# A low-rank update on one core: nine and sixteen tiles in one load each, and the first group's work dealt anew

## The chip, the cores and the metric

The kernel runs on one core of one Trainium2 chip. Its time is the device time of one execution in microseconds (us). "Before" is the median of three runs. The profile shows one further execution; its span goes from the first to the last instruction, and its device time is a little longer than the span.

## The reference

x has 16 x 512 = 8192 rows (tokens) of 768 float32 values. A is 768 x 16, B is 16 x 768, and scale is 0.5.

```python
def reference(x, A, B, scale):
    lora = np.matmul(np.matmul(x, A), B)
    return (x + scale * lora).astype(np.float32)
```

Each row of x is projected to 16 numbers by A, these are raised to 768 numbers again by B, and half of that is added to the row. x is read once and the result written once, 25.2 MB each way.

## The kernel before

**Tiles, parts, groups.** A tile is 128 rows of x. The 64 tiles are cut into five parts of 9, 7, 16, 16 and 16 tiles (`PARTS`); in a part each of the 128 partitions holds consecutive rows, so a load of a whole part takes one contiguous piece of memory per partition. x stays in `x_all` (48 tiles of room, named x_sb in the profile); the fifth part goes where the first two were, once they have been stored. The compute goes by groups of eight tiles, numbered 0 to 7, and a group is summed in four pairs of tiles.

**One group's way.** ACT and POOL each narrow four tiles of x to float16 (`narrowed`, L186 to L196, into `xn`). DVE transposes the group in blocks of 32 x 32 (`turned`, L248, into `xt`). PE projects it with 24 matmuls (`projected`, L278, into y_ps, shown as ps_yt), in two halves of 12. ACT scales and spreads the result into block-diagonal `y_bd` with four instructions (L238). PE raises each pair with four matmuls (`raised`, L293, into one of two `lora` buffers), and DVE adds the pair to x in place (`summed`, L252). In the loop on PE (L324 to L331) the order is: raise pairs 0 and 1 of a group, the first half of the next group's projection, raise pairs 2 and 3, the second half.

**Order.** Each engine's work is written out by hand in a function of its own, and semaphores join them. `s_load` counts landed loads, `s_narrow` narrowed halves, `s_turned` transposed groups, `s_taken` that PE has read weights and data of a projection's second matmul (then `xn` and `xt` may be written again), `s_y` finished projections, `s_spread` finished spreads, `s_lora` raised pairs, `s_free` pairs whose lora buffer has been read, `s_sum` the last sum of groups 1, 3, 5 and 7 (`STORED`). Since an instruction of DVE raises one semaphore, the pair behind `s_sum` gets its `s_free` from SP, in SP's `summed` (L141).

**SP issues every transfer**, in this order: load 0 (2 tiles), load 1 (7 tiles), three small loads for A, one for B, load 2 (7), loads 3 and 4 (8 each, the third part), load 5 (16). Then it waits for `s_sum` of group 1 and for ten raised pairs, that is two pairs of group 2 (L169), and issues store 0 (9 tiles) and store 1 (7). As these two land, the loads of the fifth part follow, 8 tiles each. Then come stores 2, 3 and 4 (16 tiles each), each when its groups are summed; store 2 waits besides until PE has begun to raise group 5 (`s_raise`, L181).

**The first group** is dealt by hand. POOL narrows tiles 0 and 1 as load 0 lands, ACT tiles 2 and 3 and then 4 to 7 as load 1 lands. POOL narrows B (`b_half`, L212), and PE spreads it over the partitions (L315), from which ACT makes `b_mm` (L231). DVE transposes A (L243), and POOL makes the projection's weights of it (`w_one` L214, `w_bd` L220). DVE transposes the first group in two halves (L261 to L264).

Of the kernel before, what the change touches and what calls it, by code (L numbers as in the profile page):

```python
# [13 lines left out]
PARTS = [9, 7, 16, 16, 16]  # L14


GROUP = 8

SUB = 4
# [5 lines left out]
SETS, SET = 3, 4  # L25
# [3 lines left out]
def kernel(  # L29
# [19 lines left out]
    NG = sum(PARTS) // GROUP  # L49
    PAIRS = GROUP // 2  # L50
# [4 lines left out]
    def sb(name, shape, dtype):  # L55
        return nc.alloc_sbuf_tensor(name, shape, dtype).ap()
# [13 lines left out]
    b_rows = sb("b_rows", [P, D], fp32)  # L70
    b_half = sb("b_half", [P, D], MM_DT)
# [11 lines left out]
    def sem(name):  # L83
        sems.append(nc.alloc_semaphore(name))
        return sems[-1]
# [10 lines left out]
    def memory(t2, i, s, n):  # L96
        S = PARTS[i]
        return t2[ds(parts[i], S * P), :].rearrange("(p s) d -> p s d", s=S)[:, ds(s, n), :]

    def held(i, s, n):  # L100
        return tiles(where.index((i, s)), n)

    def tiles(t, n):
        return x_all[:, ds(t % ROOM, n), :]

    LOADS = [
        (0, 0, 2), (0, 2, 7), (1, 0, 7), (2, 0, 8), (2, 8, 8), (3, 0, 16), (4, 0, 8), (4, 8, 8)
    ]
    s_load = [sem(f"s_load{k}") for k in range(len(LOADS))]

    def load_of(t):
        i, s = where[t]
        return next(k for k, ld in enumerate(LOADS) if ld[0] == i and ld[1] <= s < ld[1] + ld[2])

    assert SETS * SET == NC
    s_a, s_b = sem("s_a"), sem("s_b")
    s_ready, s_brows, s_pick = sem("s_ready"), sem("s_brows"), sem("s_pick")
    s_w, s_bh, s_bp, s_bm = sem("s_w"), sem("s_bh"), sem("s_bp"), sem("s_bm")
    s_first, s_narrow, s_turned, s_taken = sem("s_first"), sem("s_narrow"), sem("s_turned"), sem("s_taken")
    s_y, s_spread, s_lora = sem("s_y"), sem("s_spread"), sem("s_lora")  # L120

    s_free = [sem(f"s_free{p}") for p in range(PAIRS)]
    s_out0, s_out1, s_raise = sem("s_out0"), sem("s_out1"), sem("s_raise")

    s_sum, s_out = sem("s_sum"), sem("s_out")

# [1 line left out]
    STORES = [(0, 0, 9), (1, 0, 7), (2, 0, 16), (3, 0, 16), (4, 0, 16)]  # L128

    STORED = [where.index((i, s + n - 1)) // GROUP for i, s, n in STORES]  # L130
    assert STORED[0] == STORED[1]

    section = ExitStack()
    section.enter_context(tc.tile_critical(no_gpsimd_drain=True))  # L134
# [1 line left out]
    def on_sync(e):  # L136
        def load(k):
            ld = LOADS[k]
            e.dma_start(out=held(*ld), in_=memory(x2, *ld)).then_inc(s_load[k], 16)  # L139

        def summed(k):  # L141
            e.wait_ge(s_sum, sorted(set(STORED)).index(STORED[k]) + 1)
            if STORED[k] + 1 < NG:

                e.sem_inc(s_free[PAIRS - 1], 1)

        def store(k, done):
            st = STORES[k]
            e.dma_start(out=memory(out2, *st), in_=held(*st)).then_inc(done, 16)

        load(0)
        load(1)
        e.wait_ge(s_ready, 1)
        blocks = A.rearrange("(c e) r -> c (e r)", e=64)
        for c in range(SETS):
            e.dma_start(
                out=a_rows[c : SET * SET : SET, :], in_=blocks[ds(c * SET, SET), :]
            ).then_inc(s_a, 16)
        e.wait_ge(s_brows, 1)
        e.dma_start(out=b_rows[0 : R * APART : APART, :], in_=B).then_inc(s_b, 16)  # L160
        for k in range(2, len(LOADS) - 2):
            load(k)

        for p in range(2, PAIRS):
            e.sem_inc(s_free[p], 1)
        summed(0)


        e.wait_ge(s_lora, 2 * PAIRS + 2)  # L169
        store(0, s_out0)  # L170
        store(1, s_out1)
        e.wait_ge(s_out0, 16)
        load(len(LOADS) - 2)
        e.wait_ge(s_out1, 16)
        load(len(LOADS) - 1)
        for k in range(2, len(STORES)):
            summed(k)
            if k == 2:


                e.wait_ge(s_raise, 6)  # L181
            store(k, s_out)

    here = set()
# [1 line left out]
    def narrowed(e, copy, g, first, n=SUB):  # L186
        t = g * GROUP + first
        for k in dict.fromkeys(load_of(t + k) for k in range(n)):
            if (e, k) not in here:
                here.add((e, k))  # L190
                e.wait_ge(s_load[k], 16)
        if g:
            e.wait_ge(s_taken, g)
        ins = copy(out=xn[:, ds(first, n), :], in_=tiles(t, n))  # L194

        ins.then_inc(s_narrow if g else s_first if first else s_a, 1)  # L196

    def on_gpsimd(e):
        e.memset(a_rows[0:Q], 0.0).then_inc(s_ready, 1)  # L199
        e.memset(b_rows, 0.0).then_inc(s_brows, 1)  # L200
        e.memset(pick, 0.0).then_inc(s_pick, 1)
        e.memset(w_bd.rearrange("p c k m -> p (c k m)").bitcast(fp32), 0.0)  # L202
        e.memset(y_bd.rearrange("p s m -> p (s m)").bitcast(fp32), 0.0).then_inc(s_ready, 1)  # L203
        e.wait_ge(s_pick, 1)
        e.affine_select(  # L205
            out=pick, in_=pick, compare_op=mybir.AluOpType.not_equal, fill=1.0, base=0,
            pattern=[[0, NQ], [-APART, Q]], channel_multiplier=1,
        ).then_inc(s_pick, 1)
        narrowed(e, e.tensor_copy, 0, 0, SUB // 2)
        e.wait_ge(s_pick, 2)  # L210
        e.wait_ge(s_b, 16)
        e.tensor_copy(out=b_half, in_=b_rows).then_inc(s_bh, 1)  # L212
        e.wait_ge(s_ready, 3)
        e.tensor_copy(  # L214
            out=w_one.rearrange("i (c e) k r -> i c e (k r)", c=SETS),
            in_=a_t[0:Q].rearrange("i k r (e c) -> i c e (k r)", c=SET)[:, 0:SETS, 0:SET, :],
        ).then_inc(s_w, 1)
        e.wait_ge(s_w, 1)
        for b in range(NQ):
            e.tensor_copy(  # L220
                out=w_bd[ds(b * Q, Q), :, :, ds(b * Q, R)], in_=w_one
            ).then_inc(s_w, 1)
            e.wait_ge(s_w, b + 2)
        for g in range(1, NG):
            narrowed(e, e.tensor_copy, g, SUB)

    def on_scalar(e):
        narrowed(e, e.copy, 0, SUB // 2, SUB // 2)
        narrowed(e, e.copy, 0, SUB)
        e.wait_ge(s_bp, 1)  # L230
        e.copy(out=b_mm, in_=lora[0][:, 0, :]).then_inc(s_bm, 1)  # L231
        for g in range(NG):
            if g + 1 < NG:
                narrowed(e, e.copy, g + 1, 0)
            e.wait_ge(s_y, g + 1)
            for b in range(NQ):
                q = ds(b * Q, Q)
                last = e.mul(out=y_bd[q, :, q], in_=y_ps[q, :, :], mul=sc)  # L238
            last.then_inc(s_spread, 1)

    def on_vector(e):
        e.wait_ge(s_a, SETS * 16 + 1)
        e.transpose(  # L243
            out=a_t[0:Q].rearrange("i k r c -> i (k r) c"),
            in_=a_rows[0:Q].rearrange("c (i k r) -> c (k r) i", k=2, r=R),
        ).then_inc(s_ready, 1)

        def turned(first, n):  # L248
            ts = [v[:, ds(first, n), :].bitcast(fp32) for v in (xt, xn)]
            return e.transpose(out=ts[0], in_=ts[1])  # L250

        def summed(g, p):  # L252
            xs = tiles(g * GROUP + 2 * p, 2)
            e.wait_ge(s_lora, g * PAIRS + p + 1)
            ins = e.tensor_tensor(out=xs, in0=xs, in1=lora[p % 2], op=mybir.AluOpType.add)  # L255
            if p + 1 == PAIRS and g in STORED:
                ins.then_inc(s_sum, 1)
            elif g + 1 < NG or p + 2 < PAIRS:
                ins.then_inc(s_free[p], 1)

        for h in range(2):  # L261
            e.wait_ge(s_first, h + 1)
            ins = turned(h * SUB, SUB)
        ins.then_inc(s_turned, 1)  # L264
        for g in range(NG):
            if g + 1 < NG:
                e.wait_ge(s_y, g + 1)
                e.wait_ge(s_narrow, 2 * (g + 1))  # L268
                turned(0, GROUP).then_inc(s_turned, 1)
            for p in range(PAIRS):  # L270
                summed(g, p)

    def on_tensor(e):
# [19 lines left out]
        def raised(p):  # L293
            if p == 0:
                e.wait_ge(s_spread, 1)
            free = s_free[(p + 2) % PAIRS]
            e.wait_ge(free, 1)
            t = lora[p % 2]
            mms = []
            for k in range(2):  # L300
                for n0, w in ((0, 512), (512, 256)) if k == 0 else ((0, 256), (256, 512)):
                    mms.append(e.matmul(  # L302
                        t[:, k, ds(n0, w)], y_bd[:, 2 * p + k, :], b_mm[:, ds(n0, w)],
                        start=True, stop=True,
                    ))
            if p == 0:
                mms[0].then_inc(s_raise, 1)
                mms[2].then_inc(s_spread, -1)
            mms[1].then_inc(free, -1)
            mms[-1].then_inc(s_lora, 1)  # L310
# [73 lines left out]
```

## Time and profile before

| What | Value |
|---|---|
| time, median of three runs | 123.47 us (123.42 to 123.60) |
| time of the profiled execution | 123.43 us |
| its span | 121.6 us |
| read from and written to memory | 25.26 MB and 25.17 MB, 415 GB/s over the span |
| busy: DVE, PE, ACT, POOL | 67%, 41%, 31%, 23% of the span |
| one pair's sum on DVE (L255) | 1.735 us, 32 times |
| one group's transposition on DVE (L250) | 3.365 us, 7 times, and two halves of 1.75 us |
| narrowing of four tiles | 2.75 us on ACT and on POOL |
| spread of y on ACT (L238) | four instructions of 0.37 us |

Transfers by time of issue and of landing, in us of the span:

| Transfer | Tiles | Issued | Landed |
|---|---|---|---|
| load 0 | 2 | 0.97 | 5.5 |
| load 1 | 7 | 1.42 | 12.1 |
| load 2 | 7 | 4.57 | 18.6 |
| load 3 | 8 | 5.18 | 25.9 |
| load 4 | 8 | 5.66 | 33.2 |
| load 5 | 16 | 6.15 | 47.8 |
| store 0 | 9 | 44.45 | 55.9 |
| store 1 | 7 | 44.85 | 62.5 |
| load 6 | 8 | 55.95 | 69.7 |
| load 7 | 8 | 62.52 | 77.0 |
| store 2 | 16 | 74.47 | 91.5 |
| store 3 | 16 | 82.67 | 106.2 |
| store 4 | 16 | 100.64 | 120.7 |

How to read it: the busy shares are averages over the span. A transfer's issue is an instruction on SP; its bytes then go through 16 transfer engines, each with its own queue, and a transfer has landed when all 16 have reported. Where the landing of one follows the one before by the time that its bytes take, the engines had no pause between them. The clock that PE was granted stands in the profile as PEclk, in tenths of full speed or as a share; a matmul takes twice as long at half the clock.

### The profile page before, as it was taken

How to read it: one execution, taken by the hardware profiler on the slowest of the kernel's cores; microseconds unless marked ns; L12 is line 12 of the kernel's file. 1: busy time of each engine (PE TensorE's matmuls, PEld its weight loads, DVE VectorE, ACT ScalarE, POOL GpSimd, SP SyncE). 2: the span in 40 equal slices, each digit the busy share in tenths (PEclk: the TensorE clock that was granted, in tenths of full speed). 3: DMA queues.
4: the chain of work that ended last, by engine and by line, in shares of the span. 5: the costliest groups of instructions: out<-in, count | busy, mean ns of one | idle time of the engine just before them, and what ended most of it. 6: DMA issues, size and time to landing. Idle time of an engine off the chain costs nothing.

```text
span 121.6 us, 884 instructions
## 1 busy us (share of the span) xinstructions
PE 49.8 (41%) x322; PEld 29.2 (24%) x322; DVE 81.7 (67%) x42; ACT 37.4 (31%) x43; POOL 28.4 (23%) x24
## 2 busy tenths in 40 slices
PE   0000209487457547746745734774674320000000
PEld 0000006253223424424423322442442110000000
DVE  0000970599999999999999989999995990000000
ACT  4000967626408312735340093643004000000000
POOL 7730567126009002605300080620000000000000
PEclk9999999999999999999999999999999995555555
DMA  3999999999999897999999999998999899899890
GB/s 63 437 431 457 446 398 469 404 420 469 437 517 420 356 517 336 427 421 410 446 416 436 428 428 485 420 517 372 404 517 404 372 517 404 372 517 404 372 517 0
DMA packets 1928, 50.43 MB, mean 415 GB/s; under 512 B 236, under 2 KB 236, under 8 KB 392
## 3 DMA queue, kind: packets, MB, share of 16 engines
q1 hardware_dynamic: 1928, 50.43, 97.0%
HBM read 25.26 MB, written 25.17 MB: 415 GB/s over the span
## 4 chain that ended last, share of the span: by engine, by line
DVE 33%; DMA 29%; PE 9%; ACT 6%; POOL 2%; issue 2%; SPq 0%; DVEq 0%
DVE x_sb L255 21%; DMA x_sb<-in_x_dram 20%; DVE xt L250 12%; DMA out_dram<-x_sb 9%; PE ps_yt L281 6%; ACT xn L194 3%; PE lora_ps L302 3%; ACT y_bd L238 2%; POOL xn L194 2%; SPq L139 0%; SPq L379 0%; DVEq L268 0%; SPq L134 0%
## 5 line engine op out<-in xcount | busy, mean ns | idle before, releaser
L255 DVE TENSOR_TENSOR x_sb<-x_sb,lora_ps 128x1536 f32<-128x1536 f32 x32 | 53.7, 1735 | 1.4 <-PE lora_ps L302 1.4
L194 ACT CAST xn<-x_sb 128x3072 f16<-128x3072 f32 (+1 forms) x9 | 23.4, 2609 | 35.9 <-DMA x_sb<-in_x_dram 24.8
L302 PE MATMUL lora_ps<-b_mm,y_bd 128*128 128x512 f16 (+1 forms) x128 | 25.0, 328 | 22.6 <-ACT y_bd L238 14.3
L194 POOL CAST xn<-x_sb 128x3072 f16<-128x3072 f32 (+1 forms) x8 | 20.7, 2586 | 43.9 <-DMA x_sb<-in_x_dram 24.6
L250 DVE STREAM_TRANSPOSE xt<-xn 128x3072 f32<-128x3072 f32 (+1 forms) x9 | 27.1, 3006 | 5.3 <-PE ps_yt L281 4.4
L281 PE MATMUL ps_yt<-xt,w_bd 128*128 128x256 f16 x192 | 25.2, 282 | 12.2 <-DVE xt L250 12.2
L281 PEld LDWEIGHTS ps_yt<-xt,w_bd 128*128 128x128 f16 x192 | 18.5, 99 | 19.7 <-issue 15.4
L302 PEld LDWEIGHTS lora_ps<-b_mm,y_bd 128*128 128x128 f16 x128 | 10.6, 97 | 35.5 <-ACT y_bd L238 16.6
L238 ACT ACTIVATE y_bd<-ps_yt 32x256 f16<-32x256 f32 x32 | 12.0, 374 | 18.7 <-PE ps_yt L281 18.4
L243 DVE STREAM_TRANSPOSE a_t<-a_rows 32x1024 f32<-32x1024 f32 x1 | 2.0, 1955 | 12.2 <-DMA a_rows<-in_A_dram 12.2
L315 PE MATMUL lora_ps<-b_half,pick 128*128 128x512 f16 (+1 forms) x2 | 0.8, 500 | 13.5 <-POOL b_half L212 13.5
L315 PEld LDWEIGHTS lora_ps<-b_half,pick 128*128 128x128 f16 x2 | 0.1, 105 | 13.5 <-issue 13.5
L212 POOL CAST b_half<-b_rows 128x768 f16<-128x768 f32 x1 | 0.8, 827 | 5.5 <-DMA b_rows<-in_B_dram 5.5
L220 POOL COPY w_bd<-w_one 32x384 f16<-32x384 f16 x4 | 2.0, 500 | 0.2
L194 ACT ACT_TABLE_LOAD x1 | 1.3, 1283 | 0.9 <-SPq L134 0.9
L202 POOL MEMSET w_bd<- 128x1536 f32 x1 | 1.4, 1372 | 0.0
L214 POOL CAST w_one<-a_t 32x384 f16<-32x384 f32 x1 | 0.9, 857 | 0.9 <-DVE a_t L243 0.9
L199 POOL MEMSET a_rows<- 32x1024 f32 x1 | 0.9, 941 | 0.5 <-SPq L134 0.5
L231 ACT CAST b_mm<-lora_ps 128x768 f16<-128x768 f32 x1 | 0.8, 798 | 0.0
L200 POOL MEMSET b_rows<- 128x768 f32 x1 | 0.7, 728 | 0.0
L203 POOL MEMSET y_bd<- 128x512 f32 x1 | 0.5, 514 | 0.0
L205 POOL TENSOR_SCALAR_AFFINE_SELECT pick<-pick 128x128 f16<-128x128 f16 x1 | 0.3, 298 | 0.0
(5 smaller groups left out, 0.6 us busy)
## 6 DMA issues: line engine op xcount, KB each, us to landing
out_dram<-x_sb SPq DMA_DIRECT2D x3, 6144.0 KB, 20.1
x_sb<-in_x_dram SPq DMA_DIRECT2D x4, 3072.0 KB, 17.6
x_sb<-in_x_dram SPq DMA_DIRECT2D x1, 6144.0 KB, 41.6
x_sb<-in_x_dram SPq DMA_DIRECT2D x2, 2688.0 KB, 12.4
out_dram<-x_sb SPq DMA_DIRECT2D x1, 3456.0 KB, 11.5
out_dram<-x_sb SPq DMA_DIRECT2D x1, 2688.0 KB, 17.7
x_sb<-in_x_dram SPq DMA_DIRECT2D x1, 768.0 KB, 4.5
a_rows<-in_A_dram SPq DMA_DIRECT2D x3, 16.0 KB
```

The lines of the kernel that those rows point to most:

```text
L194: ins = copy(out=xn[:, ds(first, n), :], in_=tiles(t, n))
L199: e.memset(a_rows[0:Q], 0.0).then_inc(s_ready, 1)
L202: e.memset(w_bd.rearrange("p c k m -> p (c k m)").bitcast(fp32), 0.0)
L214: e.tensor_copy(out=w_one.rearrange("i (c e) k r -> i c e (k r)", c=SETS), in_=a_t[0:Q].rearrange("i k r (e c) -> i c e (k r)", c=SET)[:, ...
L220: e.tensor_copy(out=w_bd[ds(b * Q, Q), :, :, ds(b * Q, R)], in_=w_one).then_inc(s_w, 1)
L238: last = e.mul(out=y_bd[q, :, q], in_=y_ps[q, :, :], mul=sc)
L243: e.transpose(out=a_t[0:Q].rearrange("i k r c -> i (k r) c"), in_=a_rows[0:Q].rearrange("c (i k r) -> c (k r) i", k=2, r=R),).then_inc(s_r ...
L250: return e.transpose(out=ts[0], in_=ts[1])
L255: ins = e.tensor_tensor(out=xs, in0=xs, in1=lora[p % 2], op=mybir.AluOpType.add)
L281: mm = e.matmul(y_ps, w_bd[:, c, k, :], xv[:, :, c, :, k], start=(m == 0), stop=(m == MMS - 1),)
L302: mms.append(e.matmul(t[:, k, ds(n0, w)], y_bd[:, 2 * p + k, :], b_mm[:, ds(n0, w)], start=True, stop=True,))
L315: last = e.matmul(lora[0][:, 0, ds(n0, w)], pick.rearrange("p b r -> p (b r)"), b_half[:, ds(n0, w)], start=True, stop=True,)
```

## The change

- The first part's nine tiles come as one load in place of two and seven, and the third part's 16 tiles as one in place of eight and eight. There are six loads of x and not eight.
- In the first group ACT narrows tiles 0 to 3 and POOL tiles 4 to 7, one instruction each. ACT, not POOL, narrows B. DVE waits for ACT's half and then for POOL's, which now counts in `s_narrow`; so each later wait on `s_narrow` is for one more.
- On ACT, the narrowing of group 2 comes behind the spread of group 1, and not ahead of it.
- On DVE, the first pair of group 1 is summed ahead of the transposition of group 2.
- On SP, store 0 waits for the third projection (`s_y` at 3) and neither for group 1's last sum nor for raised pairs; that sum is waited for behind it, ahead of store 1. Store 2 waits for the sixth projection (`s_y` at 6), and `s_raise` is gone.

```diff
     LOADS = [
-        (0, 0, 2), (0, 2, 7), (1, 0, 7), (2, 0, 8), (2, 8, 8), (3, 0, 16), (4, 0, 8), (4, 8, 8)
+        (0, 0, 9), (1, 0, 7), (2, 0, 16), (3, 0, 16), (4, 0, 8), (4, 8, 8)
     ]
...
-    assert STORED[0] == STORED[1]
+    assert STORED[0] == STORED[1] == 1 and PARTS[0] <= GROUP + 2
...
         load(0)
-        load(1)
         e.wait_ge(s_ready, 1)
...
-        for k in range(2, len(LOADS) - 2):
+        for k in range(1, len(LOADS) - 2):
             load(k)
...
-        summed(0)
-        e.wait_ge(s_lora, 2 * PAIRS + 2)
+        e.wait_ge(s_y, 3)
         store(0, s_out0)
+        summed(1)
         store(1, s_out1)
...
-                e.wait_ge(s_raise, 6)
+                e.wait_ge(s_y, 6)
...
-        ins.then_inc(s_narrow if g else s_first if first else s_a, 1)
+        ins.then_inc(s_narrow if g or first else s_first, 1)
...
     def on_gpsimd(e):
...
-        narrowed(e, e.tensor_copy, 0, 0, SUB // 2)
-        e.wait_ge(s_pick, 2)
-        e.wait_ge(s_b, 16)
-        e.tensor_copy(out=b_half, in_=b_rows).then_inc(s_bh, 1)
+        narrowed(e, e.tensor_copy, 0, SUB)
...
     def on_scalar(e):
-        narrowed(e, e.copy, 0, SUB // 2, SUB // 2)
-        narrowed(e, e.copy, 0, SUB)
+        narrowed(e, e.copy, 0, 0)
+        e.wait_ge(s_b, 16)
+        e.copy(out=b_half, in_=b_rows).then_inc(s_bh, 1)
...
         for g in range(NG):
-            if g + 1 < NG:
+            if g + 1 < NG and g != 1:
                 narrowed(e, e.copy, g + 1, 0)
...
             last.then_inc(s_spread, 1)
+            if g == 1:
+                narrowed(e, e.copy, g + 1, 0)
...
     def on_vector(e):
-        e.wait_ge(s_a, SETS * 16 + 1)
+        e.wait_ge(s_a, SETS * 16)
...
         for h in range(2):
-            e.wait_ge(s_first, h + 1)
+            e.wait_ge(s_narrow if h else s_first, 1)
             ins = turned(h * SUB, SUB)
         ins.then_inc(s_turned, 1)
         for g in range(NG):
+            ahead = 1 if g == 1 else 0
+            for p in range(ahead):
+                summed(g, p)
             if g + 1 < NG:
                 e.wait_ge(s_y, g + 1)
-                e.wait_ge(s_narrow, 2 * (g + 1))
+                e.wait_ge(s_narrow, 2 * (g + 1) + 1)
                 turned(0, GROUP).then_inc(s_turned, 1)
-            for p in range(PAIRS):
+            for p in range(ahead, PAIRS):
                 summed(g, p)
...
             if p == 0:
-                mms[0].then_inc(s_raise, 1)
                 mms[2].then_inc(s_spread, -1)
```

More of the change, by code (lines that the diff above doesn't have):

```diff
@@ L122 @@
     s_free = [sem(f"s_free{p}") for p in range(PAIRS)]
-    s_out0, s_out1, s_raise = sem("s_out0"), sem("s_out1"), sem("s_raise")
+    s_out0, s_out1 = sem("s_out0"), sem("s_out1")
     s_sum, s_out = sem("s_sum"), sem("s_out")
```

## The prediction, made before the changed kernel was run

> **What bounds the kernel now.** I first looked at section 2 and 3 of the page, since 50 MB move through one core.
>
> ```profile
> PEclk9999999999999999999999999999999995555555
> DMA  3999999999999897999999999998999899899890
> ...
> q1 hardware_dynamic: 1928, 50.43, 97.0%
> ```
>
> The transfer engines are busy from the first slice to the last but one, while the busiest compute engine, DVE, is busy for 67%. The packet records say the same: from the first packet at 1.98 us to the first engine's end at 119.2 no engine is without one. So the span is 1.98 us of start, 118.7 us of gapless transfers (the last store lands at 120.70) and 0.9 us of tail. Whatever leaves this queue full leaves the time as it is; a hole in it is added. So I next asked how late each issue may come. All five stores and the last two loads are issued from SP while an earlier transfer still runs. The chain of waits shows which work sets them:
>
> ```profile
> 42.95 1.49 PE lora_ps L302 x8
> 44.44 0.02 issue
> 44.45 11.48 DMA out_dram<-x_sb
> 55.93 0.02 issue
> 55.95 13.71 DMA x_sb<-in_x_dram
> ...
> 93.86 6.75 DVE x_sb L255 x4
> ```
>
> Store 0 goes out at 44.45, when PE has raised two pairs of group 2; the engines run out of loads between 46.5 and 47.3 (packet records). From an issue to its packets I have one row with an empty queue: the first load, issued at 0.97, whose packets begin on the 16 engines at 1.98 to 2.4, one at 2.7. So an issue is needed 1.0 to 1.7 us ahead: store 0 by about 45.4. Store 2 goes at 74.47 (engines free from 75.7), the last at 100.64 (free from 104.7).
>
> Third, the timeline around group 1 and 2, where the change works:
>
> ```profile
> 31.44 1.53 ACT L238 ACTIVATE y_bd<-ps_yt 32x256 f16<-32x256 f32 x4 [2.18 <-PE ps_yt L281]
> ...
> 33.03 1.47 PE L302 MATMUL lora_ps<-b_mm,y_bd 128*128 128x512 f16 x8 [1.62 <-ACT y_bd L238]
> 35.73 6.71 DVE L255 TENSOR_TENSOR x_sb<-x_sb,lora_ps 128x1536 f32<-128x1536 f32 x4
> ...
> 35.95 1.50 PE L281 MATMUL ps_yt<-xt,w_bd 128*128 128x256 f16 x12 [1.45 <-DVE xt L250]
> ```
>
> DVE is the pace of the compute: a transposition (3.29 from start to start) and four sums (1.66 each) make 9.92 us a group, and PE waits for it 1.45 us. Last, PE's clock, by stretches of 3.41 us (why this width, below; the columns after the stretch are its length, the busy time and count of PE, PEld, DVE, ACT, POOL, then the granted clock):
>
> ```profile
> 72.44:75.86 3.42, 1.47 (x8) 0.70 (x8) 3.29 (x1) 1.50 (x4) 0.02 (x1) 1.00 0.95 410
> ...
> 96.34:99.75 3.41, 0.98 (x5) 0.31 (x4) 3.41 (x3) 0.00 (x0) 0.00 (x0) 1.00 0.97 418
> 99.75:103.16 3.41, 0.00 (x0) 0.00 (x0) 0.86 (x1) 0.00 (x0) 0.00 (x0) 0.50 0.97 418
> ```
>
> The clock is halved at 99.75, only 1.6 us after the last matmul ended (98.16), behind a stretch with 0.98 us of matmuls. Stretches with 1.47 us kept it. The full clock came at 21.24 (the distance between two L281 matmuls falls there from 213 to 112 ns), and from there to 99.75 are 78.51 us, 23 times 3.413: that is where my width comes from.
>
> **Part 1: fewer, larger loads.** Per engine, eight packets of 6 KB and eight of 21.5 KB (0.231 and 0.796 us each from start to start) become eight of 27.6 KB (1.022): 8.21 - 8.17 = 0.04 us. Sixteen of 24.6 KB (0.910) become eight of 49 KB (1.812): 0.06. Two completion records fewer: 0.03. Sum -0.13 us, all on the path. The first packets also cost 0.67 us per engine over their later price, the latency of an empty queue; a larger first packet may hide from none to all of it. I take none: the first packet of each engine was the slow one in nearly all cases.
>
> **Part 2: the first group dealt anew.** ACT narrows four tiles in one go (2.75) from 12.1, and POOL the other four, instead of 4.13 on ACT beside 1.46 early on POOL. ACT then makes b_half (0.80 to 0.83) and b_mm (0.80) until 17.4, before its next tile's input at 18.5. POOL ends its four at 14.9, then w_one (0.86) and w_bd (2.18): 18.0 instead of 17.35. DVE's second half-transposition can begin at 16.6 and ends at 18.4, not 18.06. So the first projection starts 0.2 us later. That delay alone costs nothing: store 0 had 0.9 us to spare.
>
> **Part 3: the third part as one load.** Its first half landed at 25.9 (issued 5.18, 20.7 to landing); now all of it lands where the second half did, 33.2 (5.66 + 27.6), less 0.1. ACT and POOL cannot narrow group 2 before (26.5 until now): 33.2 + 2.75 = 35.95. Behind ACT's narrowing stands nothing of group 1, since its spread of y is moved ahead of it (33.2). DVE sums the pair moved ahead, when raised, at 34.1 to 35.8, then transposes group 2 from 36.0 to 39.4, instead of to 35.8. Now DVE is about 3 us behind, and with the full clock everything follows: projections done at 43.6 to 43.9 (first half from 39.5, 1.5; raises 2 and 3, 0.65 each; second half 1.5), group 1 summed at 45.2, the last sum near 103.0 instead of 100.6 (0.4 us of old idle time at 72.2 taken up). The moved waits fit that: store 0 on the third projection at 43.7, store 1 at 45.2, store 2 on the sixth projection at 73.8, the last store at 103.0, all earlier than the engines run out. Behind SP's new wait stands its credit for the last pair, wanted by PE at 46. With this the sum would be 123.43 - 0.13 = 123.3.
>
> **But PE stands idle.** Its last matmul before the wait ends at 34.7 (raises 0 and 1 of group 1 from 33.25, 1.47), its next starts at 39.5: 4.8 us, with 1.6 us of idle time ahead of those raises too. The longest gap in the trace of before is 2.98 us (71.07 to 74.05). However the 3.41 us stretches fall, one of them holds under 1.0 us of matmuls here: a stretch starting between 33.7 and 37.1 does, and that is nearly a full stretch of starting points. So I expect the half clock at 39.5. At it an L281 matmul takes 213 ns for 112, so the 24 projections and 8 raises behind the transposition (4.4 us of warm work) go at half pace until a stretch was busy enough: 0.89 of one was, at 21.24. A stretch that begins in the wait ends too early to be busy enough, so this takes a whole stretch and up to part of a second from 39.5: 3.4 to 5.4 us, say 4.6, of which half is lost: 2.3 (1.7 to 2.7; 1 if the drop falls behind 39.5 or the return needs little).
>
> [...]
>
> **The sum.** (a) Third projection at 43.7 + 2.3 = 46.0, so store 0's packets at 47.0 to 47.7, the engines free at 46.4 to 47.2: a hole of 0.65 us (0 to 1.2). The first packet behind an empty queue costs more, as at the start, where it was 0.67; a store reads its first bytes from x_sb and not from memory, so between 0 and 0.67, and I take 0.3. (b) Raises 2 and 3 come late for DVE too: raise 2 ends near 43.4 (39.5 + 2.6 + 1.3) instead of 41.8, so the next sum begins 1.6 us later, and its chain is 1.1 to 1.6, say 1.5, further behind. Store 2 at 75.3, packets at 76.3 to 77.0 against engines free at 75.6 to 76.4 and, behind (a), 0.95 later: nothing, up to 0.3. (c) Last sum at 103.0 + 1.5 = 104.5, packets 105.5 to 106.2, against 104.6 to 105.4 and 0.95 later: 0.15 on average (0 to 0.5), since the engine that is served last need not be the one that is free last. Together 0.65 + 0.3 + 0.15 = 1.1, less 0.13: +1.0 us. The profiled execution took 123.43 (span 121.6 and 1.83 around it), 0.04 under the median of 123.47. **Forecast: 124.4 us**, own range 123.75 to 125.6 (from no hole but the late last store, to 5.4 us of half clock, the slow end of 1.0 to 1.7 us and 0.67 for the first packets).
>
> **Rivals.** Measurements of this kernel tell 0.2%, 0.25 us, from no change.
> 1. The clock stays full, or is back within 2 us, so that store 0 is in time. It stays full if only a stretch without any matmul halves it: 4.8 us hold a whole one of 3.41 for (4.8 - 3.41) / 3.41 = 41% of the places where it can begin, so most executions would miss it. For it: the bound between 0.98 and 1.47 us rests on one drop. Against it: that drop came behind a stretch with matmuls. Then 123.3, within 0.2%; 15%.
> 2. The other side: the same, and the larger first packets hide the start. Per engine 0.67 us is at stake; 0.13 + 0.2 to 0.67 gives 122.6 to 123.1, faster. It decides once over 0.12 us of the start is saved. For it: second packets were also slow on four engines (609 to 993 ns for 234), as if small packets outran their descriptors. Against: first packets alone hold most of it; 15%.
> 3. The clock stays low through the whole of the 4.4 us of work: third projection at 43.7 + 4.4 = 48.1, the hole at store 0 is 2.8 us, with the first packet 3.1, less 0.13: 126.4. It decides if the return needs a busier stretch than the 0.89 at 21.24, and PE's half-speed work for a group (10.2 us against DVE's 9.92) would supply that; 8%, counted with slower.
>
> **How the numbers follow.** Forecast 62%, rival 3 8%: slower 70%; same 15%, faster 15%. The range 123.1 to 125.6 leaves out most of rival 2 and of 3.
>
> **What would show it.** L281 matmuls near 213 ns apart around 40 us and two more clock changes; L250's transposition of group 2 at 36.0 to 39.4; store 0's issue near 46.0; a slice around 47 us with a low DMA share; the last sum near 104.5. I am wrong if the clock stays full through 40 us, if a store issued that late still finds its engines busy, or if the first load lands well before 11.9.

## The result, and the profile after

| | before | changed |
|---|---|---|
| median of the runs | 123.55 us (123.42 to 123.6, 6 runs) | 125.25 us (124.21 to 126.22, 6 runs) |
| ratio, 95% interval | | 1.0104 [1.0078, 1.013] |
| profiled execution | 123.43 us | 125.27 us |
| last store lands, in the span | 120.70 us | 122.41 us |

The changed kernel is slower by 1.0%, 1.3 us. The comparison leaves disturbed runs out, so its ratio lies below that of the medians. The runs of the changed kernel lie at 124.2 to 124.3 and at 125.2 to 125.3 (one at 126.22); the trace is of 125.27, so what it explains is 1.84 us, of which 1.71 is the later landing of the last store.

First the page of the changed kernel: the granted clock and the busy share of the transfer engines in 40 slices of 3.08 us, and the queue's share.

```profile
PEclk9999999999999689999999999999999999655555
DMA  4998999899799986999989999979997996996990
...
q1 hardware_dynamic: 1640, 50.43, 96.3%
```

The queue carries the same 50.43 MB in 288 packets fewer, and is full for 96.3% of a longer span. Packets are counted where they start, so a low slice is only a hint. The packet records do not name the engine, but each packet can be followed to the next by its end; by them the 6 of the sixteenth slice (46.2 to 49.3 us) is a hole, while in the two 6s near the end (slices 34 and 37) no engine stands empty. Just ahead of the hole the clock falls, in the fourteenth slice. The timeline of the changed kernel (start, busy time, engine, operation, and in brackets the idle time ahead and what ended it) shows what leads there:

```profile
19.16 5.00 PE L285 MATMUL ps_yt<-xt,w_bd 128*128 128x256 f16 x24 [1.94 <-DVE xt L250]
...
33.13 1.53 ACT L235 ACTIVATE y_bd<-ps_yt 32x256 f16<-32x256 f32 x4 [7.40 <-PE ps_yt L285]
33.88 2.75 POOL L193 CAST xn<-x_sb 128x3072 f16<-128x3072 f32 x1 [11.23 <-DMA x_sb<-in_x_dram]
34.68 2.75 ACT L193 CAST xn<-x_sb 128x3072 f16<-128x3072 f32 x1
...
37.54 3.38 DVE L250 STREAM_TRANSPOSE xt<-xn 128x3072 f32<-128x3072 f32 x1 [0.21 <-ACT xn L193]
...
41.06 2.72 PE L285 MATMUL ps_yt<-xt,w_bd 128*128 128x256 f16 x12 [4.88 <-DVE xt L250]
...
44.74 3.42 DVE L255 TENSOR_TENSOR x_sb<-x_sb,lora_ps 128x1536 f32<-128x1536 f32 x2 [2.19 <-PE lora_ps L306]
...
46.72 1.88 SPq L149 DMA_DIRECT2D out_dram<-x_sb  x2
```

PE waits 4.88 us for the transposition of group 2, and the 12 matmuls behind that wait take 2.72 us, for 1.50 with the full clock. DVE then waits another 2.19 us for raised pairs. The third projection ends at 46.69, and SP issues store 0 at 46.72, 2.3 us later than before. Windows of one clock stretch each (length, busy time and count of PE, PEld, DVE, ACT, POOL, granted clock, DMA share, GB/s), and one of the hole:

```profile
37.39:40.80 3.41, 0.00 (x0) 0.00 (x0) 3.26 (x1) 0.04 (x1) 0.00 (x0) 1.00 1.07 461
40.80:44.21 3.41, 3.15 (x14) 2.08 (x15) 1.76 (x2) 2.52 (x1) 2.49 (x1) 0.50 1.03 447
...
46.00:47.00 1.00, 0.69 (x7) 0.36 (x4) 1.00 (x2) 0.27 (x1) 0.00 (x0) 1.00 0.12 49
```

A whole stretch passes without a matmul; the next one is granted half the clock, and the one behind it the full clock again. From 46 to 47 only 49 GB/s move. By the packet records 15 of the transfer engines stand empty there for 0.36 to 1.18 us; the sixteenth, the last to finish its loads (47.92), does not pause. The mean of the 16 is 0.72. A second loss does not show as a hole. At 60.6 to 63 us the engines turn from store 1 to the load behind it, and their packets there take 0.87 us more than usual (mean of the 16 engines; before 0.16):

```profile
61.00:62.00 1.00, 0.49 (x5) 0.46 (x6) 1.00 (x2) 0.07 (x1) 0.04 (x1) 1.00 1.42 344
62.00:63.00 1.00, 1.00 (x10) 0.62 (x7) 1.00 (x2) 1.00 (x1) 1.00 (x1) 1.00 0.65 221
```

Those two rows carry 344 and 221 GB/s; the same two microseconds of before carry 436 and 418. Since packets are counted where they start, a share may pass 1.

The 1.71 us are then: the start 0.15 later, the hole 0.72, the turn 0.72 more than before, a small hole at 77 us 0.07, fewer packets -0.13, and 0.18 that these terms leave over. (It is no wider spread of the engines' ends: they lie 0.58 us apart, for 1.02 before.) The compute side gives the same answer. The last sum ends at 105.87, 5.26 us later than before: 1.68 from the start (the first projection is that much later at its end), and 3.77 from DVE's three waits (1.37, 0.21, 2.19), less 0.2 of old idle time. The last store was issued at 105.90, some 1.1 us before the engines had worked off what stood ahead of it: the lateness had eaten the spare time, and no hole was left to make there.

### The profile page after: what moved, and what is told of

It reads as the page before. It is cut to its first block, busy times and chain, and to the rows that moved or that the text cites. A ratio compares the mean times of both kernels' runs of the same rounds, so it can differ in the third digit from the quotient of the medians.

```text
span 123.3 us, 878 instructions
## 1 busy us (share of the span) xinstructions
PE 51.7 (42%) x322; PEld 30.5 (25%) x322; DVE 81.9 (66%) x42; ACT 36.8 (30%) x43; POOL 28.8 (23%) x23
## 2 busy tenths in 40 slices
DMA packets 1640, 50.43 MB, mean 409 GB/s; under 512 B 204, under 2 KB 204, under 8 KB 232
## 3 DMA queue, kind: packets, MB, share of 16 engines
q1 hardware_dynamic: 1640, 50.43, 96.3%
## 4 chain that ended last, share of the span: by engine, by line
DVE 54%; PE 11%; DMA 10%; ACT 7%; issue 4%; SPq 0%; DVEq 0%
DVE x_sb L255 32%; DVE xt L250 22%; DMA x_sb<-in_x_dram 10%; PE ps_yt L285 8%; ACT xn L193 4%; PE lora_ps L306 3%; ACT y_bd L235 2%; SPq L382 0%; DVEq L272 0%; SPq L134 0%
## 5 line engine op out<-in xcount | busy, mean ns | idle before, releaser
L193 POOL CAST xn<-x_sb 128x3072 f16<-128x3072 f32 x8 | 22.0, 2746 | 54.8 <-PE ps_yt L285 35.6
L285 PE MATMUL ps_yt<-xt,w_bd 128*128 128x256 f16 x192 | 27.2, 296 | 14.9 <-DVE xt L250 14.9
L193 ACT CAST xn<-x_sb 128x3072 f16<-128x3072 f32 x8 | 22.0, 2752 | 30.8 <-PE ps_yt L285 20.2
L285 PEld LDWEIGHTS ps_yt<-xt,w_bd 128*128 128x128 f16 x192 | 19.5, 104 | 23.1 <-issue 18.1
L226 ACT CAST b_half<-b_rows 128x768 f16<-128x768 f32 x1 | 0.8, 826 | 0.0
```

Source lines behind the costliest of these rows:

```text
L285: mm = e.matmul(y_ps, w_bd[:, c, k, :], xv[:, :, c, :, k], start=(m == 0), stop=(m == MMS - 1),)
```

## The experiments

Each kernel is named with its ratio to the kernel before; one per cent is 1.23 us. "After" is the changed kernel.

**Which part makes group 2 late?** Four edits of after, e1 to e4: the third part as two loads again; the first nine tiles as two loads again; PE kept busy through the long wait; store 0 waiting for raised pairs instead of the third projection.

```diff
-        (0, 0, 9), (1, 0, 7), (2, 0, 16), (3, 0, 16), (4, 0, 8), (4, 8, 8)
+        (0, 0, 9), (1, 0, 7), (2, 0, 8), (2, 8, 8), (3, 0, 16), (4, 0, 8), (4, 8, 8)
```

> The changed kernel with the third part loaded as 8 and 8 tiles again; all else of the change stays. Theory 'PE's wait' (the wait for the whole third part lets PE's clock drop, and the late third projection opens a hole at store 0): group 2's first half lands near 26, PE never waits over 3 us, the clock stays full, no hole, 123.3 to 123.6 us. Theory 'start' (the larger first load and the first group dealt anew cost most of the 1.7 us): still 124.5 or more, first load's landing near 12.8.

Measured: 124.97 us, 1.0107 [1.004, 1.0174]: nothing regained that stands clear of the scatter. The timeline of this kernel says why.

```profile
27.95 2.75 POOL L193 CAST xn<-x_sb 128x3072 f16<-128x3072 f32 x1 [5.71 <-PE ps_yt L285]
...
32.83 1.54 ACT L235 ACTIVATE y_bd<-ps_yt 32x256 f16<-32x256 f32 x4 [7.40 <-PE ps_yt L285]
...
34.40 2.75 ACT L193 CAST xn<-x_sb 128x3072 f16<-128x3072 f32 x1
...
37.25 3.38 DVE L250 STREAM_TRANSPOSE xt<-xn 128x3072 f32<-128x3072 f32 x1 [0.21 <-ACT xn L193]
```

The data is there early now: POOL narrows its half at 27.95, as soon as `xn` is free. ACT had 7.40 us without work, and still narrowed its half at 34.40, since its new order puts the spread of group 1 first. DVE started at 37.25 (after: 37.54), the clock halved at 40.63, and the hole was 0.51 us. The landing and the new order each make group 2 late by about as much, and undoing one leaves the other. The expectation, which had only the landing, fell.

```diff
-        (0, 0, 9), (1, 0, 7), (2, 0, 16), (3, 0, 16), (4, 0, 8), (4, 8, 8)
+        (0, 0, 2), (0, 2, 7), (1, 0, 7), (2, 0, 16), (3, 0, 16), (4, 0, 8), (4, 8, 8)
...
         load(0)
+        load(1)
         e.wait_ge(s_ready, 1)
...
-        for k in range(1, len(LOADS) - 2):
+        for k in range(2, len(LOADS) - 2):
             load(k)
```

> The changed kernel with the first nine tiles loaded as 2 and 7 again; the third part stays one load. Theory 'PE's wait': the clock still drops behind group 1, hole at store 0, 124.2 to 125.3 us. Theory 'start': first nine tiles land near 12.1, no more than 123.8 us.

Measured: 125.56 us, 1.0164 [1.0124, 1.0203]. The first tiles landed at 11.93 for 12.77, yet the last sum ended at 106.05 and the hole was 1.07 us. That does not clear the start, for ACT's timeline shows that the start came no earlier:

```profile
12.01 1.28 ACT L194 ACT_TABLE_LOAD   x1 [12.01 <-DMA x_sb<-in_x_dram]
...
13.30 2.75 ACT L194 CAST xn<-x_sb 128x3072 f16<-128x3072 f32 x1
```

In this kernel ACT loads its table (1.28 us) only behind the landing; in after it does so at 0.91 us. Its narrowing starts at 13.30 for 12.79, and the first projection at 19.67 for 19.16. What the start is worth is read from e11 below.

```diff
+        def step(extra=0):
             raised(0)
             raised(1)
+            for _ in range(extra):
+                e.matmul(warm_ps, w_bd[:, 0, 0, :], b_mm[:, 0:256], start=True, stop=True)
             e.wait_ge(s_turned, 1)
...
+        step()
+        step(36)
+        with e.Fori(2, NG - 1):
+            step()
```

The 36 extra matmuls write a tile that nobody reads.

> The changed kernel; behind raises 0 and 1 of group 1 PE does 36 further matmuls of 128x256 into an unused part of PSUM (4.0 us at full clock), ahead of its wait for group 2's transposition; the first two groups of the loop are written out for it. It adds work and takes no wait away. Theory 'PE's wait, through the clock': clock full from its first rise until the end, L285 matmuls 112 ns apart behind the wait, third projection about 1.3 us earlier (45.3 if the start is as in the profile of the changed kernel), hole at store 0 under 0.3 us, last sum 1.3 us earlier: 123.4 to 124.0 us. Theory 'lateness alone' (the third part's landing makes DVE late, and the clock adds nothing): 124.7 us or more, as without the matmuls.

Measured: 125.22 us, 1.0152 [1.0123, 1.0182], for the 123.4 to 124.0 of the clock's theory. The clock stayed full to 100.9 us, the third projection ended at 44.36, the last sum at 103.54, and no hole was left. But the longer program brought a loss of its own, which the page of this kernel lists as a second queue:

```profile
q8 instruction: 1, 0.02, 0.1%
```

That one packet of 16,384 bytes, at 39.4 us, took 1.07 us of one transfer engine, and one engine (taken for the same; the records do not name it) ended at 121.67. The other 15 ended at 119.2 to 120.2, as the engines of before did. So the run shows what the clock does to PE, and but for one engine the queue is back at its old end; the time does not show what that is worth.

```diff
-        e.wait_ge(s_y, 3)
+        e.wait_ge(s_lora, PAIRS + 3)
         store(0, s_out0)
```

> The changed kernel with store 0 waiting for seven raised pairs (pair 2 of group 1, by which group 1's first pair is summed) and not for the third projection: its issue comes near 44.8 and not 46.7, while PE's clock still drops. Theory 'hole at store 0 alone': the engines stay fed, 123.4 to 123.7 us. Theory 'two limits at once' (the last sum is late too, and 16.5 us lie between the last store's issue and its landing): no hole near 47, but one of about 1.5 us near 106, and 124.7 to 125.2 us.

Measured: 124.73 us, 1.008 [1.0046, 1.0114]. Store 0 went out at 44.80 and the hole at 47 us was gone; a hole of 1.31 us came in its place at store 2 (the expectation had it at the last store). The trace is of 125.14, the longest of six executions from 123.96 on. A window of this kernel, columns as above:

```profile
76.00:77.00 1.00, 0.87 (x8) 0.50 (x6) 1.00 (x2) 0.10 (x1) 0.00 (x0) 1.00 0.12 49
```

This fits a compute that is late by more than the stores can spare: the lateness is charged where it first leaves the queue empty.

**The order, with and without the rest.** e5 is e1 with ACT's and DVE's old order, so that the merged first load, the first group's new dealing and the moved store waits remain (store 0 waits for group 1's last sum besides). e6 is the kernel before with the new order and the moved waits alone (the change's own hunks on ACT, DVE and SP); the order without the moved waits was not run. e5, against e1:

```diff
-            if g + 1 < NG and g != 1:
+            if g + 1 < NG:
                 narrowed(e, e.copy, g + 1, 0)
...
-            if g == 1:
-                narrowed(e, e.copy, g + 1, 0)
...
-            ahead = 1 if g == 1 else 0
+            ahead = 0
...
+        summed(1)
         e.wait_ge(s_y, 3)
         store(0, s_out0)
-        summed(1)
```

> The changed kernel with the third part as 8 and 8 tiles, and with the old order on ACT (narrowing of group 2 ahead of group 1's spread) and on DVE (no pair summed ahead); store 0 waits for group 1's last sum and the third projection. What stays of the change: the nine-tile load, the first group dealt anew, the moved waits. Theory 'order': splitting the third part alone left 125.0 us because ACT's narrowing still stood behind the spread; with the order back PE waits 1.5 us and no more, the last sum comes 1.0 to 2.4 us later than before, inside the 3.5 us that the last store had to spare: 123.3 to 123.7 us. Theory 'start': the late first group is what costs, 124.3 us or more.

> The kernel before with the changed order on ACT and DVE and the changed waits of the stores; its loads and its first group stay. Theory 'order': DVE's idle time of 1.4 and 0.2 us ahead of group 2's transposition and, with PE's clock halved, about 2.2 us behind it make the last sum 3.5 to 4.5 us late, just past what there is to spare: 123.5 to 124.6 us, the clock halved once between 36 and 41 us. Theory 'the loads are needed for it': 123.3 to 123.6 us and a full clock.

Measured: e5 124.16 us, 1.0051 [1.0035, 1.0066], between its two theories; e6 124.10 us, 1.0053 [1.0036, 1.007], as the order's theory had it. In e6 ACT narrows group 2 at 33.51, and its timeline goes on, with the old loads, as the changed kernel's does:

```profile
36.36 3.38 DVE L250 STREAM_TRANSPOSE xt<-xn 128x3072 f32<-128x3072 f32 x1 [0.21 <-ACT xn L192]
...
39.89 2.40 PE L284 MATMUL ps_yt<-xt,w_bd 128*128 128x256 f16 x12 [4.88 <-DVE xt L250]
```

The same 4.88 us on PE, and the clock halved from 40.28 to 43.70; here store 0 at 45.71 was just in time, without a hole, and the packets at the turn from store to load at 60 us took 0.76 us more than usual. In e5 all of that is gone (PE waits 1.45 us, the last sum ends at 101.29; the clock is halved later, from 74.61 to 78.03), and it is still 0.5% slower; its trace is of 124.54, the longest of ten executions. It issued store 0 at 43.69, earlier than the kernel before (44.45), and the loads' packets around 45 us were slower by 0.30 us an engine. That gave a theory that I had not had: a store that is issued too early costs as well.

**The clock, without a longer program.** e7: in the loop of after, in turn 1 alone, 36 matmuls into an unread tile:

```diff
-        with e.Fori(0, NG - 1):
+        with e.Fori(0, NG - 1) as i:
             raised(0)
             raised(1)
+            with e.If(i == 1):
+                with e.Fori(0, 9):
+                    for _ in range(4):
+                        e.matmul(warm_ps, w_bd[:, 0, 0, :], b_mm[:, 0:256], start=True, stop=True)
```

> The changed kernel; in the loop's second turn PE does nine times four further matmuls of 128x256 into an unused part of PSUM ahead of its wait for group 2's transposition, as an inner loop, so that PE's program stays short (the written-out form of this run fetched 16 KB of program at 39.4 us through one transfer engine's queue, and that engine ended 1.5 us behind the others). Theory 'clock': full clock from its first rise on, no packet of 16384 bytes, last sum 1.5 to 2.5 us earlier than without the matmuls (103.4 to 104.4), no hole at store 0 or store 2 over 0.2 us: 123.3 to 123.8 us. Theory 'lateness without the clock': 124.5 us or more.

Measured: 125.4 us, 1.0183 [1.0136, 1.023], from 124.1, 125.18, 125.62 and 126.4 (the medians' ratio is 1.0157). The trace is of the 124.1; its timeline is:

```profile
39.60 1.50 PE L286 MATMUL ps_yt<-xt,w_bd 128*128 128x256 f16 x12 [0.95 <-DVE xt L251]
...
41.78 3.42 DVE L256 TENSOR_TENSOR x_sb<-x_sb,lora_ps 128x1536 f32<-128x1536 f32 x2 [0.69 <-PE lora_ps L307]
```

The extra matmuls kept PE busy for 4.09 us from 34.56; the projection takes 1.50 us and DVE waits 0.69 for 2.19. From the start of the transposition to the end of the third projection are 7.65 us (36.08 to 43.73), for 9.15 in after: the half clock costs 1.5 us of lateness. By that alone the changed kernel's store 0 would go at 45.2, and e6, with 45.71, had no hole. The rest by which e7 is earlier (2.96 us at the end of the third projection) is its start: the same code ended the first projection at 22.69, for 24.16 in after's trace.

No hole is left in this execution, the turn at 60 us costs 0.16 us, and the last store lands at 120.83: 1.58 us earlier than after's, 0.13 later than before's. So nearly all of the 1.71 us is regained inside the span, which is 121.7 us for before's 121.6. The time is longer for what lies outside the span, 2.4 us for 1.8. The four spans are 121.7, 121.7, 123.2 and 123.1 us, with 2.4 to 3.5 us outside; the other kernels have 1.7 to 2.0. What lies there, and what makes two of the spans long, no trace shows. The expectation of 123.3 to 123.8 us failed, and what the full clock is worth in time stays open.

**Both late stores freed.** e10 is e4, and store 2 no longer waits for the sixth projection:

```diff
             summed(k)
-            if k == 2:
-                e.wait_ge(s_y, 6)
             store(k, s_out)
```

> The changed kernel with store 0 waiting for seven raised pairs (as in the run with the earlier store 0) and store 2 for its sums alone. Theory 'the stores' waits': without holes at store 0 and store 2 the time is 123.4 to 123.8 us. Theory 'last sum': both holes go, but the last sum stays near 105.9 with the clock halved, and a hole of 1 to 1.7 us opens at the last store (packets from 106.9, engines free from 105.2): 124.6 to 125.2 us.

Measured: 124.38 us, 1.0075 [1.0058, 1.0092]. The clock halved from 39.73 to 43.14. Store 0 went at 43.78 and store 2 at 67.14; the first hole now was at the last store, behind a last sum at 104.92, of 0.29 us; 1 to 1.7 were expected, and 124.6 us or more. The trace is of 123.87, the shortest of four executions (the others 124.34 to 124.44). What the last store left over was paid around the early ones: slow load packets of 0.41 us near 45 us and 0.13 near 75.

**The parts alone.** e11 is e5 with the store waits put back to the old times; against before, it holds the nine-tile load and the first group's new dealing alone. e12 is before with nothing but the two store waits moved (issues at 43.01, behind group 1's last sum, and 71.58), e14 with store 0's alone (42.46), e13 before with the third part as one load alone.

e11, against e5:

```diff
         summed(1)
-        e.wait_ge(s_y, 3)
+        e.wait_ge(s_lora, 2 * PAIRS + 1)
         store(0, s_out0)
...
-                e.wait_ge(s_y, 6)
+                e.wait_ge(s_raise, 6)
```

e12, against before (e14 is the first of the two alone):

```diff
         summed(0)
-        e.wait_ge(s_lora, 2 * PAIRS + 2)
+        e.wait_ge(s_y, 3)
         store(0, s_out0)
...
-                e.wait_ge(s_raise, 6)
+                e.wait_ge(s_y, 6)
```

e13, against before:

```diff
-        (0, 0, 2), (0, 2, 7), (1, 0, 7), (2, 0, 8), (2, 8, 8), (3, 0, 16), (4, 0, 8), (4, 8, 8)
+        (0, 0, 2), (0, 2, 7), (1, 0, 7), (2, 0, 16), (3, 0, 16), (4, 0, 8), (4, 8, 8)
```

> The run with the order undone, with store 0 waiting for nine raised pairs (near 44.9, as late as in the kernel before) and store 2 for the sixth raise again. Of the change only the nine-tile load and the first group dealt anew stay. Theory 'early stores' (a store issued over 2 us before its loads are through slows the loads' last packets, which cost 0.29 us of all engines near 45 and 0.29 near 75 in that run): no slow packets there, 123.3 to 123.6 us. Theory 'start': 124.0 us or more, as in that run.

> The kernel before with the two moved waits alone: store 0 goes at group 1's last sum (near 42.5) instead of 44.45, store 2 at the sixth projection (near 71.1) instead of 74.47. Nothing else is changed. Theory 'early stores': slow load packets near 44 to 46 and 73 to 76, 0.3 to 0.5 us of all engines at each, 123.9 to 124.4 us. Theory 'a queue in order does not care when a store is queued': 123.4 to 123.6 us.

> The kernel before with the wait of store 0 alone moved (issue near 42.5 and not 44.45); store 2 keeps its wait. Theory 'early stores': one of the two losses, 0.2 to 0.5 us, 123.65 to 124.0 us, slow packets near 44 to 46 and none near 75. Other theory: 123.4 to 123.6 us.

> The kernel before with the third part as one load of 16 tiles, and nothing else. Theory 'PE's wait': ACT narrows group 2 at 33.2 to 36.0 ahead of group 1's spread, so group 1's raises come near 37.6 and PE is idle for 6 us; the clock drops once, the third projection comes near 45.5 and store 0, behind two raised pairs, near 48.6: a hole of 2 to 3 us, last sum near 105.5, 125.3 to 126.5 us. Rival: the packets saved are all that counts, 123.4 us.

| alone, against before | us | ratio | in us |
|---|---|---|---|
| e11: nine-tile load, first group | 123.68 | 1.002 [1.001, 1.0031] | +0.25 |
| e12: both store waits | 124.10 | 1.0052 [1.0039, 1.0065] | +0.64 |
| e14: store 0's wait | 124.02 | 1.0047 [1.0034, 1.006] | +0.58 |
| e6: order and store waits | 124.10 | 1.0053 [1.0036, 1.007] | +0.65 |
| e13: third part as one load | 126.46 | 1.0242 [1.0226, 1.0257] | +3.0 |
| all of the change | 125.25 | 1.0104 [1.0078, 1.013] | +1.3 |

e12 and e13 lie in the ranges expected; e11 and e14 lie 0.08 and 0.02 us above theirs. The early store is plainest in e14, beside e11 with the same stretch and store 0 at 44.46. First e14, then e11:

```profile
43.00:44.00 1.00, 1.00 (x8) 0.59 (x6) 1.00 (x1) 0.00 (x0) 0.00 (x0) 1.00 0.73 295
44.00:45.00 1.00, 0.35 (x3) 0.00 (x0) 1.00 (x1) 0.00 (x0) 0.00 (x0) 1.00 2.01 590
45.00:46.00 1.00, 0.21 (x2) 0.22 (x3) 1.00 (x2) 0.00 (x0) 0.00 (x0) 1.00 0.68 197
```

```profile
43.00:44.00 1.00, 0.40 (x3) 0.27 (x4) 1.00 (x2) 0.54 (x2) 0.00 (x0) 1.00 1.25 541
44.00:45.00 1.00, 1.00 (x7) 0.43 (x5) 1.00 (x1) 0.00 (x0) 0.00 (x0) 1.00 1.02 442
45.00:46.00 1.00, 0.08 (x1) 0.00 (x0) 1.00 (x1) 0.00 (x0) 0.00 (x0) 1.00 0.82 344
```

In three microseconds e14 moves 1,082 KB and e11 1,327 KB (the sum of the last column, at 1 us a row). The 245 KB are 0.6 us at the 410 to 415 GB/s of these pages, about the price that e14 measured; the count is rough, since a packet of 49 KB counts whole where it starts. The packet records say where it goes: in e12 the last load packet of each of the 16 engines, with the store already queued behind it, took 0.4 to 1.3 us longer. By the time of store 0's issue, the slow packets of the loads cost per engine 0.92 us (42.46, e14), 0.90 (43.01, e12), 0.30 (43.69, e5), 0.46 (43.76, e7), 0.41 (43.78, e10), and at most 0.04 in before, e11 and e4 (44.45, 44.46, 44.80). The time is less than the 0.92 of e14, in part because its turn at 60 us cost 0.01 us, for 0.16 in before. For store 2 it is weaker: 0.30 at 72.25 (e5), but 0.05 at 71.58 (e12).

e13 has the merged load without the new order. Its timeline, and then the windows of its hole:

```profile
32.95 2.75 ACT L194 CAST xn<-x_sb 128x3072 f16<-128x3072 f32 x1 [8.17 <-DMA x_sb<-in_x_dram]
...
35.72 1.53 ACT L238 ACTIVATE y_bd<-ps_yt 32x256 f16<-32x256 f32 x4
...
37.31 2.74 PE L302 MATMUL lora_ps<-b_mm,y_bd 128*128 128x512 f16 x8 [5.18 <-ACT y_bd L238]
...
43.23 1.50 PE L281 MATMUL ps_yt<-xt,w_bd 128*128 128x256 f16 x12
...
47.85 0.82 SPq L149 DMA_DIRECT2D out_dram<-x_sb  x2
```

```profile
46.00:47.00 1.00, 0.65 (x4) 0.41 (x5) 1.00 (x1) 0.30 (x1) 0.00 (x0) 1.00 0.01 0
47.00:48.00 1.00, 0.82 (x5) 0.29 (x3) 1.00 (x1) 0.00 (x0) 0.00 (x0) 1.00 0.00 0
```

Here ACT waits 8.17 us for the load, in front of group 1's spread, so group 1 itself is held up: PE is idle for 5.18 us, raises at half clock (2.74 us for 1.47), and store 0, which here still waits for raised pairs of group 2, leaves at 47.85. The hole is 2.1 us. So the merged load is the costliest part when it comes alone. It is not the new order that makes the whole change cheaper: e13, with the old order, ended its third projection at 44.73 and its last sum at 104.51, while the changed kernel ended them at 46.69 and 105.87, of which 1.0 us is its later start (first projection 24.16 for 23.20). By the trace it is the moved wait: on the third projection e13's store 0 could have gone 3.1 us earlier than it did. The merged load with the moved wait and the old order was not run. The parts do not add: in the whole change the late third projection also holds store 0 back, so the price of an early store, all of e12, does not arise.

## Why the prediction was right, and where it was not

- **The bound.** Right: the changed kernel's time is the queue's, and what was added is a hole and slow packets in it.
- **PE stands idle and the clock halves.** Right in place: PE waits 4.88 us for 4.8, and one stretch of half clock follows, 3.41 us from 40.80 to 44.21. (The text had this width from one interval of 78.51 us, taken as 23 stretches; the changed kernel shows a single one.) The size was too large: by e7 it is 1.5 us of lateness, below the 2.3 (1.7 to 2.7) of the text. The third projection ended at 46.69 for 46.0 all the same, because the start made up for it: 46.69 is the 43.7 of the full clock, 1.5 for the clock, and 1.5 by which the start was late beyond the text's 0.2.
- **(a)** The hole at store 0: 0.72 us for 0.65, which is in part luck. With the start of the text and the clock's 1.5 us store 0 would have gone near 45.2, where e6 suggests no hole. The 0.3 for the first packets behind it was wrong: they took no longer than others.
- **(b), (c)** Store 2's hole was 0.07 for "nothing, up to 0.3"; the last store's was none, for 0.15. Part 1's -0.13 was met by the packet records.
- **The sum was mis-sized**, +1.0 for +1.84 in the profiled execution, in two terms. The start was costed at 0.2 us on compute and nothing on the queue. In the trace the nine-tile load landed 0.67 us later than load 0 and 1 had (12.77 for 12.10), the full clock came 2.49 us later (23.73 for 21.24), so that the first projection took 5.00 us for 4.26; transfers lost 0.15. Most of this belongs to the one execution. One engine's first packet began at 3.38 us, the other 15 by 2.93, and it ended its share of the load at 12.29, the others by 11.54; in e5 and e7 the same load landed at 12.04 and 12.06. In e7 the full clock came at 21.42 and the first projection ended 0.2 us behind before's, as the text had it. By e11 the start alone is worth 0.25 us. And the turn from store to load at 60 us, 0.72 us above before's, was no term of the sum at all.
- **"Behind ACT's narrowing stands nothing of group 1"** named the landing as the one cause of group 2's lateness, and costed the order at nothing under it. e1 takes this cover away: with the old loads the order gives the same 4.88 us and the same half clock. The text has no price for the order with the cover gone.
- **"The moved waits fit that: … all earlier than the engines run out"** took earlier as free. e12 and e14 show +0.6 us for it.
- **Rival 1** (full clock, 123.3) did not come true, but its price was nearly right: in the traced execution of e7, with a full clock and no hole, the last store landed 0.13 us after before's, for 0.13 ahead of it in the text, with store 0 at 43.76 and 0.46 us of slow load packets. Its condition, that only a stretch without any matmul halves the clock, no run shows: the clock fell behind 0.82 us of matmuls in a stretch (changed kernel, 105.65), 0.98 (before, 99.75), 1.35 (e4, 37.97) and 1.41 (e14, 72.99). **Rival 2** (larger first packets hide the start) is refuted: first packets took 1.0 to 2.3 us for 1.025, and the load landed at 12.04 to 12.77 in the runs with it; that small packets outrun their descriptors was a guess, and no trace shows a descriptor. **Rival 3** failed on its condition: the clock was back after one stretch. In e4 it was not, from 37.97 to 44.80, yet the third projection ended at 46.84 and not at 48.1, since the stretch began before the work did.

Open: what separates the runs near 124.2 from those near 125.2 (an earlier start would do it, or stretches of the clock that fall otherwise; only traced executions could show it), and why the turn at 60 us costs at most 0.17 us in some executions and 0.5 to 0.9 in others. That is as much as the hole, so two fifths of the traced loss have a place and no cause. Most of the large values come where the 16 engines come to store 1 within half a microsecond, but e4 (0.5 us, engines 0.8 us apart) does not fit, and it was not tried.

None of the kernels tried beats the one before; the nearest, e11, is 0.2% slower.

## What to carry to other kernels

A tile is late for the slower of two reasons, its landing and its place in an engine's own order: price an edit to either with the other taken away. Before two loads become one, look for the engine that idles until the later landing; here 3 us came from one merge that saved 0.06 us of packets. Issue a store into a full queue late enough that the loads ahead of it are nearly through, and about a microsecond before the engines run empty (before's first load took 1.0 to 1.7 us from its issue to its first packets): here 44.45 was right, 42.5 and 47.85 both cost. Before a difference in the start is put down to an edit, compare the starts of several executions: here the same code ended its first projection anywhere from 22.69 to 24.16 us.

## What the runs showed of the hardware that was not expected

**A store issued early slowed the loads ahead of it**, as above: by 0.92 us an engine with the issue at 42.46 (e14), and by at most 0.04 with the issue at 44.45 to 44.80 (before, e11, e4).

**The clock fell behind stretches that held matmuls, and did not return behind every stretch that held some.** In the changed kernel it changed at 23.73, 40.80, 44.21 and 105.65 us, so 17.07, 3.41 and 61.44 us apart, which is 5, 1 and 18 times 3.413. Windows of e14 around another drop:

```profile
69.58:72.99 3.41, 1.41 (x13) 0.97 (x11) 2.53 (x2) 2.81 (x2) 2.75 (x1) 1.00 0.99 425
72.99:76.41 3.42, 1.89 (x6) 0.89 (x7) 3.37 (x2) 1.45 (x4) 0.00 (x0) 0.50 1.05 453
76.41:79.82 3.41, 3.41 (x17) 2.19 (x15) 3.31 (x3) 2.03 (x1) 1.99 (x1) 0.50 0.97 418
```

Behind 1.41 us of matmuls in a stretch the clock fell (in before and in the changed kernel stretches with 1.47 us kept it); behind 1.89 it did not come back, behind 3.41 it did (79.82). In e12 2.71 us brought it back. The drops and returns followed here lie 3.41 us apart in the changed kernel, e1, e6 and e10, 6.83 in e4 and e14. At the half clock 12 matmuls of a projection took 2.77 us (e14, from 77.06), at the full one 1.50. The late start in the changed kernel's trace goes with this: counted back from 23.73, the stretch 16.90 to 20.31 held 1.47 us of matmuls, and the matmuls behind it still took 418 ns for 271; the next held 3.42, and the clock was full at its end. In before 3.03 us in the stretch 17.83 to 21.24 were enough.

**e3's longer program came with a transfer of its own in mid-run**: with matmuls written out, it shows one packet of 16,384 bytes on a queue of the kind "instruction", which took 1.07 us, and one engine ended 1.4 us behind the next. e7, with the same matmuls in a loop, shows no such packet.
